# Loading the first chunk of a softmax in four parts instead of two

## The chip, the cores and the metric

The kernel runs on one core of a Trainium2 chip. A core has compute engines with a queue of instructions each (here VectorE, written DVE; ScalarE, ACT; GpSimd, POOL; and SyncE, SP, which here only issues transfers) and 16 DMA engines that move data between device memory (HBM) and the on-chip memory (SBUF, 128 partitions). The metric is the time of one execution on the device in microseconds; lower is better. Times of a kernel are given as the median of several runs.

## The reference

The input is 16 x 1024 rows of 512 float32 numbers. Each row gets a softmax at temperature 0.5:

```python
temp = 0.5
x_scaled = x / temp
x_max = np.max(x_scaled, axis=-1, keepdims=True)
exp_x = np.exp(x_scaled - x_max)
return (exp_x / np.sum(exp_x, axis=-1, keepdims=True)).astype(np.float32)
```

33.55 MB are read and 33.55 MB written.

## The kernel before

The 16384 rows are cut into C = 8 chunks of 2048 rows. In a chunk, each of the 128 partitions holds G = 16 successive rows of 512 numbers, 32 KB, which lie together in HBM as well. A chunk is 4 MB. Six chunks fit in SBUF (`BUFS`, line 42); chunks 6 and 7 reuse the memory of chunks 0 and 1, so their loads wait for those chunks' stores.

Transfers and computing are cut differently. `LOADS` (line 38) says in which groups of rows a chunk is loaded, `BLOCKS` (line 39) in which groups it is computed. Chunk 0 is loaded in two parts (rows 0 to 3, rows 4 to 15) and computed in three blocks (rows 0 to 3, 4 to 7, 8 to 15). The middle chunks are loaded and computed whole. Chunk 7 is loaded without its last row, which the GpSimd queue loads later (`load_last_row`, lines 88 to 100), and computed in two blocks. Every chunk is stored whole, by one DMA from the ACT queue (line 148).

For a block, `shift` (line 71) has DVE take the maximum of every row, negated (line 77), and double it (line 81). `exponentials` (line 102) has ACT compute exp(2x - 2max) for one row per partition at a time and add it up (line 108). `scale_vector` (line 120) has DVE take reciprocals of the sums (line 125) and multiply the rows by them (line 127); in blocks of eight rows or more, one row in eight is scaled by ACT instead (line 138). `store` (line 144) stores a chunk once its last block is scaled.

The order is written out by hand (lines 154 to 172). DVE's order is: maxima of block 0, maxima of block 1, then for each block i its scaling, and the maxima of block i + 2. Loads are issued by SP from within `shift`, the first time that a chunk is touched; as nothing holds the loads of chunks 0 to 5, SP issues them one after the other at the start. A reduction waits for every load that wrote something it reads: before the change, block 0 waits for the first part of chunk 0, blocks 1 and 2 for the second.

At the end an SP instruction (line 174) collects the completion of every transfer in `finished`.

Of the kernel before, what the change touches and what calls it, by code (L numbers as in the profile page):

```python
# [1 line left out]

# [4 lines left out]


@with_exitstack
def kernel(  # L10
    ctx: ExitStack,
    tc: tile.TileContext,
    x: bass.AP,
    out: bass.AP,
):
    nc = tc.nc
    fp32 = mybir.dt.float32
    P = nc.NUM_PARTITIONS
    AX = mybir.AxisListType.X
    EXP = mybir.ActivationFunctionType.Exp  # L20
    COPY = mybir.ActivationFunctionType.Copy
    MAX = mybir.AluOpType.max

    D = x.shape[-1]
    xf = x.flatten_outer_dims()
    of = out.flatten_outer_dims()
    N = xf.shape[0]

    G = 16
    C = N // (P * G)
    assert C * P * G == N
    xr = xf.rearrange("(c p g) d -> c p g d", p=P, g=G)
    outr = of.rearrange("(c p g) d -> c p g d", p=P, g=G)
    WHOLE = [(0, G)]
    LOADS = [[(0, 4), (4, G)]] + [WHOLE] * 6 + [[(0, G - 1)]]
    BLOCKS = [[(0, 4), (4, 8), (8, G)]] + [WHOLE] * 6 + [[(0, 8), (8, G)]]
    STORES = [WHOLE] * 8  # L40
    BMAX = 16
    BUFS = 6

    data = ctx.enter_context(tc.tile_pool(name="data", bufs=BUFS))
    stats = ctx.enter_context(tc.tile_pool(name="stats", bufs=6))

    ctx.enter_context(tc.manual_schedule())


    warm = stats.tile([P, 1], fp32, name="warm", bufs=1)  # L50
    nc.vector.memset(warm, 0.0)  # L51
    nc.scalar.activation(out=warm, in_=warm, func=EXP)  # L52

    chunks = {}
    blocks = [(c, lo, hi) for c in range(C) for lo, hi in BLOCKS[c]]
    n = len(blocks)
    biases, sums, recips = {}, {}, {}

    finished = []

    def load(c):
        if c < BUFS:
            chunks[c] = data.tile([P, G, D], fp32, name="xt")
        else:
            chunks[c] = chunks[c - BUFS]
        xt = chunks[c]
        for lo, hi in LOADS[c]:
            part = nc.sync.dma_start(out=xt[:, lo:hi, :], in_=xr[c][:, lo:hi, :])  # L68
            finished.append(part.ins.name)

    def shift(i):
        c, lo, hi = blocks[i]
        if c not in chunks:
            load(c)
        b = hi - lo
        negmax = stats.tile([P, BMAX], fp32, name="negmax")
        nc.vector.tensor_reduce(  # L77
            negmax[:, 0:b], chunks[c][:, lo:hi, :], axis=AX, op=MAX, negate=True
        )
        biases[i] = stats.tile([P, BMAX], fp32, name="bias")  # L80
        nc.vector.tensor_scalar_mul(biases[i][:, 0:b], negmax[:, 0:b], 2.0)  # L81

    def load_last_row(signal):
        seen = stats.tile([P, 1], fp32, name="seen", bufs=1)
        copied = nc.gpsimd.tensor_copy(out=seen, in_=signal)  # L90
        finished.append(copied.ins.name)
        c = C - 1
        halves = "p (h d) -> p h d"
        to = chunks[c - BUFS][:, G - 1, :].rearrange(halves, h=2)
        of_ = xr[c][:, G - 1, :].rearrange(halves, h=2)
        for p0, p1 in ((P - 2, P), (0, P - 2)):
            part = nc.gpsimd.dma_start(  # L97
                out=to[p0:p1], in_=of_[p0:p1], max_dma_last_dim=2 * D
            )
            finished.append(part.ins.name)  # L100

    def exponentials(i, rows):
        c, lo, hi = blocks[i]
        if i not in sums:
            sums[i] = stats.tile([P, BMAX], fp32, name="sums")
        for g in rows:
            row = chunks[c][:, lo + g, :]
            nc.scalar.activation(  # L108
                out=row,
                in_=row,  # L110
                func=EXP,
                bias=biases[i][:, g : g + 1],
                scale=2.0,
                accum_out=sums[i][:, g : g + 1],
            )
            if c == BUFS - 1 and g == 10:
                load_last_row(sums[i][:, g : g + 1])


    def scale_vector(i):  # L120
        c, lo, hi = blocks[i]
        b = hi - lo
        k = b - b // 8
        recips[i] = stats.tile([P, BMAX], fp32, name="recip")
        nc.vector.reciprocal(recips[i][:, 0:b], sums[i][:, 0:b])  # L125
        rows = chunks[c][:, lo : lo + k, :]
        last = nc.vector.tensor_mul(  # L127
            rows, rows, recips[i][:, 0:k].unsqueeze(2).broadcast_to((P, k, D))
        )
        if i == n - 1:  # L130
            finished.append(last.ins.name)

    def scale_scalar(i):
        c, lo, hi = blocks[i]
        b = hi - lo
        for g in range(b - b // 8, b):
            row = chunks[c][:, lo + g, :]
            last = nc.scalar.activation(  # L138
                out=row, in_=row, func=COPY, scale=recips[i][:, g : g + 1]
            )  # L140
            if i == n - 1:
                finished.append(last.ins.name)

    def store(i):
        c, _, end = blocks[i]
        for lo, hi in STORES[c]:
            if hi == end:
                part = nc.scalar.dma_start(
                    out=outr[c][:, lo:hi, :], in_=chunks[c][:, lo:hi, :]
                )  # L150
                if c < C - 1:
                    finished.append(part.ins.name)

    shift(0)
    shift(1)

    def rows(i):
        c, lo, hi = blocks[i]
        cut = hi - lo - (2 if c == 1 else 0)
        return range(cut), range(cut, hi - lo)  # L160

    exponentials(0, rows(0)[0])
    for i in range(n):
        if i + 1 < n:
            exponentials(i + 1, rows(i + 1)[0])
        scale_vector(i)
        scale_scalar(i)
        if i + 2 < n:
            shift(i + 2)
        store(i)  # L170
        if i + 1 < n:
            exponentials(i + 1, rows(i + 1)[1])

    seen = nc.sync.nop()
    info = mybir.DependencyInfo(
        mybir.DependencyClass.Sync, mybir.DependencyReason.DATA
    )
    for name in finished:
        tc.add_manual_dep(seen.ins, name, info, reason="leaves one wait for the end")


# [1 line left out]
_INS = ['x']  # L183
_OUTS = [((16, 1024, 512), 'float32')]


# [23 lines left out]
```

## Time and profile before

| what | value |
|---|---|
| median of 3 runs | 161.78 us (161.74 to 161.98) |
| the profiled execution | 162.29 us, span 160.5 us |
| DVE busy | 134.6 us |
| ACT busy | 102.2 us |
| bytes moved | 67.13 MB, mean 418 GB/s |
| first load, 1 MB: issue to landing | 4.8 us |
| second load, 3 MB: issue to landing | 11.6 us |

The span runs from the first instruction to the last of one execution; the time of the execution contains a little more. A page of the profile gives the busy time of each engine, the span in 40 slices with the busy share in tenths, the DMA queues (q1 is SP's, q10 ACT's, q0 GpSimd's), and the chain of waits that ended last. A "releaser" after an arrow is what ended an engine's wait. A number like L77 is a line of the kernel. A 128x4 in an instruction is partitions by elements.

### The profile page before, as it was taken

The numbers are of one execution on the slowest core, as the hardware profiler recorded it, in microseconds if no ns is written. First come the engines' busy times: TensorE is split into PE (matmuls) and PEld (weight loads), VectorE is DVE, ScalarE is ACT, GpSimd is POOL, SyncE is SP. The second block draws the span as 40 slices with busy tenths as digits, with TensorE's granted clock in tenths as the row PEclk, the third lists the DMA queues.
The fourth block names the chain that finished last, engine by engine and source line by source line (L and its number), as shares of the span: only waits on it lengthen the run. The fifth ranks groups of instructions, "written<-read, shape, count | busy, mean of one in ns | idle before, by whom it ended". The sixth has DMA issues, their size and how long they took to land.

```text
span 160.5 us, 411 instructions
## 1 busy us (share of the span) xinstructions
DVE 134.6 (84%) x45; ACT 102.2 (64%) x273; POOL 1.9 (1%) x7
## 2 busy tenths in 40 slices
DVE  0607999999999999999999999999999999957000
ACT  3071549069989963998199909991899891790000
POOL 0000000000000000000000000030000000000000
DMA  5999999999989999999999999989999999999994
GB/s 184 470 408 498 400 392 457 457 392 402 506 269 425 490 392 400 506 400 392 490 425 392 474 434 392 490 383 483 422 450 400 400 465 441 392 457 449 400 441 204
DMA packets 2578, 67.13 MB, mean 418 GB/s; under 512 B 328, under 2 KB 328, under 8 KB 400
## 3 DMA queue, kind: packets, MB, share of 16 engines
q1 hardware_dynamic: 1296, 33.29, 49.3%
q10 hardware_dynamic: 1152, 33.55, 48.4%
q0 software_dynamic: 128, 0.26, 0.4%
q14 instruction: 2, 0.02, 0.0%
HBM read 33.55 MB, written 33.55 MB: 418 GB/s over the span
## 4 chain that ended last, share of the span: by engine, by line
DVE 75%; DMA 7%; issue 5%; ACT 3%; SPq 0%
DVE negmax L77 42%; DVE xt L127 31%; DMA xt<-in_x_dram 7%; ACT xt L108 3%; DVE bias L81 1%; DVE recip L125 1%; SPq L68 0%
## 5 line engine op out<-in xcount | busy, mean ns | idle before, releaser
L108 ACT ACTIVATE xt<-xt,bias 128x512 f32<-128x512 f32 x128 | 90.4, 708 | 41.5 <-DVE bias L81 40.6
L77 DVE TENSOR_REDUCE negmax<-xt 128x16 f32<-128x8192 f32 (+2 forms) x11 | 69.9, 6352 | 9.4 <-DMA xt<-in_x_dram 9.4
L127 DVE TENSOR_TENSOR xt<-xt,recip 128x7168 f32<-128x7168 f32 (+2 forms) x11 | 62.0, 5637 | 0.4
L108 ACT ACTIVATION_READ_ACCUMULATOR xt<-xt,bias 128x1 f32 x128 | 23.9, 187 | 0.0
L138 ACT ACTIVATE xt<-xt,recip 128x512 f32<-128x512 f32 x15 | 9.9, 706 | 0.0
L125 DVE RECIPROCAL recip<-sums 128x16 f32<-128x16 f32 (+2 forms) x11 | 2.4, 218 | 1.8 <-ACT xt L108 1.8
L81 DVE TENSOR_SCALAR bias<-negmax 128x16 f32<-128x16 f32 (+2 forms) x11 | 1.9, 173 | 0.4
L52 ACT ACT_TABLE_LOAD x1 | 1.3, 1283 | 0.7 <-PEq L194 0.7
L97 POOL DMA_DIRECT2D xt<-in_x_dram x2 | 1.5, 741 | 0.5 <-issue 0.5
L90 POOL COPY seen<-sums 128x1 f32<-128x1 f32 x1 | 0.2, 184 | 103.6 <-ACT xt L108 103.6
L51 DVE MEMSET warm<- 128x1 f32 x1 | 0.1, 59 | 0.8 <-PEq L194 0.8
L52 ACT ACTIVATE warm<-warm 128x1 f32<-128x1 f32 x1 | 0.2, 202 | 0.0
L194 POOL MEMSET const-float32-0.0<- 128x1 f32 x1 | 0.1, 93 | 0.2 <-issue 0.2
L194 POOL MEMSET const-bfloat16-1.0<- 128x1 bf16 x1 | 0.1, 95 | 0.0
L194 POOL MEMSET const-uint8-127<- 128x1 uint8 x1 | 0.1, 95 | 0.0
L194 POOL MEMSET const-float32-1.0<- 128x1 f32 x1 | 0.1, 93 | 0.0
## 6 DMA issues: line engine op xcount, KB each, us to landing
out_dram<-xt ACTq DMA_DIRECT2D x8, 4096.0 KB, 23.1
xt<-in_x_dram SPq DMA_DIRECT2D x6, 4096.0 KB, 34.8
xt<-in_x_dram SPq DMA_DIRECT2D x1, 3840.0 KB, 27.8
xt<-in_x_dram SPq DMA_DIRECT2D x1, 3072.0 KB, 11.6
xt<-in_x_dram SPq DMA_DIRECT2D x1, 1024.0 KB, 4.8
xt<-in_x_dram POOLq DMA_DIRECT2D x1, 252.0 KB, 15.4
xt<-in_x_dram POOLq DMA_DIRECT2D x1, 4.0 KB, 9.1
```

Source lines behind the costliest of these rows:

```text
L51: nc.vector.memset(warm, 0.0)
L52: nc.scalar.activation(out=warm, in_=warm, func=EXP)
L77: nc.vector.tensor_reduce(negmax[:, 0:b], chunks[c][:, lo:hi, :], axis=AX, op=MAX, negate=True)
L81: nc.vector.tensor_scalar_mul(biases[i][:, 0:b], negmax[:, 0:b], 2.0)
L90: copied = nc.gpsimd.tensor_copy(out=seen, in_=signal)
L97: part = nc.gpsimd.dma_start(out=to[p0:p1], in_=of_[p0:p1], max_dma_last_dim=2 * D)
L108: nc.scalar.activation(out=row, in_=row, func=EXP, bias=biases[i][:, g : g + 1], scale=2.0, accum_out=sums[i][:, g : g + 1],)
L125: nc.vector.reciprocal(recips[i][:, 0:b], sums[i][:, 0:b])
L127: last = nc.vector.tensor_mul(rows, rows, recips[i][:, 0:k].unsqueeze(2).broadcast_to((P, k, D)))
L138: last = nc.scalar.activation(out=row, in_=row, func=COPY, scale=recips[i][:, g : g + 1])
L194: nc = _bacc.Bacc("TRN2", target_bir_lowering=False, num_devices=1)
```

## The change

The first chunk gets a list of loads of its own, in which a load may take some of the partitions only. In order: partitions 0 to 15 with rows 0 to 7 (16 KB each); partitions 16 to 127 with rows 0 to 3 (8 KB each); partitions 16 to 127 with rows 4 to 15 (24 KB each); partitions 0 to 15 with rows 8 to 15 (16 KB each). The blocks that are computed stay as they are, so block 0 (rows 0 to 3) now reads what the first two loads wrote, block 1 (rows 4 to 7) what the first and the third wrote, and block 2 (rows 8 to 15) what the third and the fourth wrote. All other loads are as before.

```diff
-    LOADS = [[(0, 4), (4, G)]] + [WHOLE] * 6 + [[(0, G - 1)]]
+    LOADS = [WHOLE] * 7 + [[(0, G - 1)]]
     BLOCKS = [[(0, 4), (4, 8), (8, G)]] + [WHOLE] * 6 + [[(0, 8), (8, G)]]
     STORES = [WHOLE] * 8
+    FIRST = [(0, 16, 0, 8), (16, P, 0, 4), (16, P, 4, G), (0, 16, 8, G)]
...
         xt = chunks[c]
-        for lo, hi in LOADS[c]:
-            part = nc.sync.dma_start(out=xt[:, lo:hi, :], in_=xr[c][:, lo:hi, :])
+        parts = FIRST if c == 0 else [(0, P, lo, hi) for lo, hi in LOADS[c]]
+        for p, q, lo, hi in parts:
+            part = nc.sync.dma_start(
+                out=xt[p:q, lo:hi, :], in_=xr[c][p:q, lo:hi, :]
+            )
             finished.append(part.ins.name)
```

## The prediction

> **What bounds the kernel now.** I read the page first for what is full, then the chain of waits, then stretches of the span at both ends.
>
> ```profile
> span 160.5 us, 411 instructions
> ...
> DVE 134.6 (84%) x45; ACT 102.2 (64%) x273; POOL 1.9 (1%) x7
> ...
> DMA  5999999999989999999999999989999999999994
> ...
> q1 hardware_dynamic: 1296, 33.29, 49.3%
> q10 hardware_dynamic: 1152, 33.55, 48.4%
> q0 software_dynamic: 128, 0.26, 0.4%
> ...
> DVE 75%; DMA 7%; issue 5%; ACT 3%; SPq 0%
> ```
>
> The chain names DVE for 75% of the span, but the queue lines say more: their packets fill 49.3 + 48.4 + 0.4 = 98.1% of the span of 16 DMA engines. One engine's rate follows from the store queue: 33.55 MB / (0.484 x 16 x 160.5 us) = 27.0 GB/s, so 16 engines make 432 GB/s and the kernel's 67.1 MB cannot take less than 67.1 / 0.432 = 155.3 us. The span is 160.5.
>
> ```profile
> core 0: us, DVE busy (x) ACT busy (x) POOL busy (x), PEclk, DMA share, GB/s
> 1.00:2.00 1.00, 0.00 (x0) 1.00 (x1) 0.00 (x0) 1.00 0.66 106
> 2.00:3.00 1.00, 0.00 (x0) 0.22 (x2) 0.00 (x0) 1.00 0.58 197
> 3.00:12.00 9.00, 2.46 (x2) 2.93 (x8) 0.00 (x0) 1.00 1.01 432
> ...
> 148.00:158.00 10.00, 0.00 (x0) 0.00 (x0) 0.00 (x0) 1.00 1.05 455
> 158.00:160.50 2.50, 0.00 (x0) 0.00 (x0) 0.00 (x0) 1.00 0.00 0
> ```
>
> The second to last column is the DMA share (packets that straddle an edge make it pass 1). The engines start at about 1.7 us, are slow for one microsecond, full from 3 us, and full again up to 158 us, when all computing has ended. What they lose anywhere in between moves the end by as much.
>
> ```profile
> 5.52 2.29 DVE L77 TENSOR_REDUCE negmax<-xt 128x4 f32<-128x2048 f32 x1 [4.65 <-DMA xt<-in_x_dram]
> ...
> 12.80 2.29 DVE L77 TENSOR_REDUCE negmax<-xt 128x4 f32<-128x2048 f32 x1 [4.79 <-DMA xt<-in_x_dram]
> ...
> 17.61 4.41 DVE L77 TENSOR_REDUCE negmax<-xt 128x8 f32<-128x4096 f32 x1
> ...
> 24.55 8.68 DVE L77 TENSOR_REDUCE negmax<-xt 128x16 f32<-128x8192 f32 x1
> ...
> 147.48 0.34 ACTq L148 DMA_DIRECT2D out_dram<-xt  x1
> ```
>
> This is the timeline (start, duration). DVE waits twice, for the two loads of the first chunk, and then runs without a gap over 0.1 us from 12.80 to 137.3 us. The last store is issued at 147.48. The store before it lands between 148.8 and 150.0 us (landings of its 16 engines), so the engines are still busy with it, and DVE's path has little slack, between nothing and about 1 us. So two paths end nearly together: the DMA's total work, and DVE from 12.80 us on. The first is the later one.
>
> [...]
>
> **The change part by part.**
>
> Removed: two loads of 128 partitions, 1.05 and 3.15 MB. Added: four loads, 0.26 MB (16 partitions x 16 KB), 0.92 MB (112 x 8 KB), 2.75 MB (112 x 24 KB), 0.26 MB (16 x 16 KB). Bytes are the same. Only chunk 0's loads change; everything else keeps its place in its queue.
>
> Issue. SP issues two more DMAs at about 0.4 us each (the row of line 68: 327 / 425 / 667 ns minimum, median, maximum), ahead of the loads of chunks 1 to 5. Chunk 1's load goes out about 0.85 us later, near 2.5 us, and its data is not due before 12 us. Hidden. The second part goes out near 1.15 us, before the first part's data flows at 1.74. Hidden. Two more completion marks per engine: taken as nothing, below 0.1 us.
>
> Part 1. At full rate 0.26 MB takes 0.61 us. [...] Lower bound: [...]0, and even a gain[...]; that gain cannot pass the slow start, which is 0.65 us (at 27.0 GB/s an engine's first 64 KB would take 2.4 us, its data ran from 1.74 to about 4.85, so 3.1 less 2.4). I take +1.8.
>
> Parts 2 and 3. Seven partitions an engine; which ones no run shows. The nearest assumption is seven in a row: engine e has 16 + 7e to 22 + 7e. [...] At full rate the parts take 3.67 MB / 0.432 = 8.5 us: +1.8 us on average[...], +3.6 us for the worst. Lower bound 0. Upper bound: neighbouring partitions handed to different engines in turn[...], +25 us. [...]
>
> Part 4. As part 1 if the engines come to it together, +1.8; less if parts 2 and 3 have set them apart: about +1.0. I take +1.4 on average, +1.0 beside the worst engine's delay.
>
> Sum for the DMA engines: 1.8 + 1.8 + 1.4 = +5.0 us on average, 1.8 + 3.6 + 1.0 = +6.4 us for the worst engine. Every later load and store of 128 partitions gives each engine equal work, so a late engine stays late to the end and the end waits for the last. [...] I take +5.4.
>
> DVE's path. The first reduce now needs parts 1 and 2: 1.8 us of part 1, 0.3 us for 0.13 MB more, and a share of part 2, so it starts near 8 us instead of 5.52. It and its exponentials (until 10.98 before) had 1.8 us to spare before 12.80, and the second reduce moves too. The second needs parts 1 to 3 and no longer part 4: 12.80 + 1.8 + 1.8 - 0.6 (0.26 MB not waited for) = 15.8, up to 17.5 behind the worst engine. That is +3.0 to +4.7, and the last store is issued by that much later; the engines are free for it 5.0 to 6.4 us later. So the DMA engines stay the later path. The third reduce needs part 4, before at 17.61, now 20.6 or later, with part 4 in by about 18.1 on average (12.8 + 5.0, and a little): covered. Chunk 1 would land near 22.5 + 5.4 = 27.9 for a reduce due at 24.55 + 3.9 = 28.5: just covered, and if not, DVE only moves closer to the DMA path.
>
> Against the profiled execution: 160.5 + 5.4 = 165.9 us span; its time is 162.29 us, 1.8 beyond the span, so 167.7. The median of the runs, 161.78, is 0.5 below: **167.2 us**.
>
> **Rivals.**
>
> A, forecast, 0.47: [...]166.0 to 168.6.
>
> B, 0.27: [...] 161.8 + 1.8 + (1.0 to 1.8) = 164.6 to 165.4; smaller still, 163, if half of that is absorbed. [...]
>
> C, not slower, 0.19: [...] Then the bytes are the same and full engines leave room for the start alone[...]. That also moves DVE's start from 12.80 to 12.2, so its path would not stand in the way. 161.2 to 161.8, with 161.4 in the middle. It decides as soon as part 1's data is through in under about 1.2 us from its first packet. For it: the 1 us at 106 and 197 GB/s is a real loss. [...]
>
> D, 0.04: partitions in turn over the engines, 190 us.
>
> E, 0.03: the split does not do what it says because the second reduce still waits for all four loads: it adds 0.6 us to DVE's path only, and A's time stands, at 167.
>
> **How the numbers follow.** Likeliest: 167.2. The range leaves out C and D, 0.23, but takes a little of the soft side of B: 162.9 to 169.6. What the measurement can tell from no change is 0.2%, 0.3 us. Slower: A, B, D, E, and 0.01 of C: 0.82. The rest of C splits into 0.13 faster and 0.05 within.
>
> **What would show it.** Right: the first reduce starts at 7.5 us or later, the second at 15 to 17.5 us; DMA in the stretch 3 to 12 us well under 432 GB/s while its share stays near 1; the last store issued near 151. Parts 2 and 3 alone: the second load's landing beyond 2.1 us after the first's. Wrong: the second reduce at 12.2 to 12.8 us with 432 GB/s from 3 us on; then C holds, and what decides is how soon the engines fill before 3 us.

## The result, and the profile after

The changed kernel takes 169.75 us (median of 5 runs, 169.41 to 170.2), the kernel before 161.78 us. The ratio is 1.0496, 95% interval 1.0475 to 1.0517: 8.0 us slower. The prediction had the direction right, and that these loads of a part of the partitions are slow, but the size too small: it said 167.2 us, and the measured time lies just above its range. Its charges for the four loads (+1.8 us for part 1, +1.8 to +3.6 for parts 2 and 3, +1.4 for part 4) were its author's estimate; no trace of the kernel before shows such loads.

The page after, with the lines that answer those of before:

```profile
span 167.5 us, 415 instructions
...
DVE 134.6 (80%) x45; ACT 102.2 (61%) x273; POOL 1.9 (1%) x7
...
DMA  6999999898999999999999999989899999999994
GB/s 102 291 270 280 184 438 438 383 493 376 471 407 462 415 438 438 430 438 399 477 391 477 391 469 399 477 383 470 384 440 476 391 462 415 454 422 430 446 422 196
...
q1 hardware_dynamic: 1328, 33.29, 51.3%
q10 hardware_dynamic: 1152, 33.55, 46.4%
...
DVE 72%; DMA 11%; issue 5%; ACT 3%; SPq 0%
```

No compute engine works longer than before: DVE still 134.6 us, ACT 102.2. The digits of the DMA row are as full as before. The row below them tells the difference: slices 2 to 5 (4.2 to 21 us) move 184 to 291 GB/s with the engines marked busy. So DMA engines that are marked busy need not move data at their full rate. The same in stretches; the last two columns are DMA share and GB/s:

```profile
core 0: us, DVE busy (x) ACT busy (x) POOL busy (x), PEclk, DMA share, GB/s
1.00:2.00 1.00, 0.00 (x0) 1.00 (x1) 0.00 (x0) 1.00 0.59 115
2.00:3.00 1.00, 0.00 (x0) 0.22 (x2) 0.00 (x0) 1.00 0.96 180
3.00:12.00 9.00, 2.46 (x2) 1.18 (x3) 0.00 (x0) 1.00 1.04 273
12.00:22.00 10.00, 2.53 (x3) 1.80 (x7) 0.00 (x0) 1.00 1.00 249
22.00:46.00 24.00, 23.83 (x10) 14.53 (x41) 0.00 (x0) 1.00 1.00 432
```

From 3 to 12 us, 273 GB/s stand where there were 432; from 22 us on, when loads of 128 partitions are all that is left, the rate is 432 again. The timeline of the reductions and of the last store:

```profile
8.30 2.29 DVE L83 TENSOR_REDUCE negmax<-xt 128x4 f32<-128x2048 f32 x1 [7.43 <-DMA xt<-in_x_dram]
...
19.43 2.29 DVE L83 TENSOR_REDUCE negmax<-xt 128x4 f32<-128x2048 f32 x1 [8.64 <-DMA xt<-in_x_dram]
...
24.24 4.41 DVE L83 TENSOR_REDUCE negmax<-xt 128x8 f32<-128x4096 f32 x1
...
31.18 8.68 DVE L83 TENSOR_REDUCE negmax<-xt 128x16 f32<-128x8192 f32 x1
...
154.11 0.34 ACTq L154 DMA_DIRECT2D out_dram<-xt  x1
```

The second reduction starts at 19.43 us instead of 12.80, and everything DVE does afterwards keeps that distance: the last store is issued at 154.11, 6.63 us later. The store before it lands between 155.8 and 157.0 us on its 16 engines, so the engines are still behind DVE, as predicted.

Landings of the last engine say how much each part cost. Part 1 landed at 5.12 us. At full rate it would have landed at 5.50 - 1.82 = 3.68, since before 1.05 MB landed at 5.50 and 0.79 MB less takes 1.82 us less: +1.4. Part 2 came 3.08 us after it, for 2.12 at full rate; part 3 11.21 us later, for 6.37; together +5.8. Part 4 came 2.06 us after that, for 0.61: +1.45. Chunk 1 followed in 9.36 us, for 9.71: -0.35. The sum is +8.3, and chunk 1 lands at 30.83 us, before at 22.51.

### The profile page after: what moved, and what is told of

Same layout as the page of the kernel before. It is cut to its first block, busy times and chain, and to the rows that moved or that the text cites. A ratio compares the mean times of both kernels' runs of the same rounds, so it can differ in the third digit from the quotient of the medians.

```text
span 167.5 us, 415 instructions
## 1 busy us (share of the span) xinstructions
DVE 134.6 (80%) x45; ACT 102.2 (61%) x273; POOL 1.9 (1%) x7
## 4 chain that ended last, share of the span: by engine, by line
DVE 72%; DMA 11%; issue 5%; ACT 3%; SPq 0%
DVE negmax L83 40%; DVE xt L133 30%; DMA xt<-in_x_dram 11%; ACT xt L114 3%; DVE bias L87 1%; DVE recip L131 1%; SPq L72 0%
```

## The experiments

**Only the number and sizes of the loads (four_wide).** Kernel before, chunk 0 in four loads over all partitions:

```diff
-    LOADS = [[(0, 4), (4, G)]] + [WHOLE] * 6 + [[(0, G - 1)]]
+    LOADS = [[(0, 1), (1, 4), (4, 15), (15, G)]] + [WHOLE] * 6 + [[(0, G - 1)]]
```

> Chunk 0 in four loads of about the same sizes as the change (1, 3, 11 and 1 rows), but each over all 128 partitions. If the narrow partition ranges are what costs: within 0.5 us of before (161.8). If the number of loads, their issue or a small first load costs: at least 2 us slower.

Measured: 162.64 us against 161.83, ratio 1.0052 (1.0033 to 1.007). The count, the issue and a small first load together cost 0.8 us here, a little more than the 0.5 expected (the interval starts at 0.53), and far less than the change's 8.0. If costs add, which was not tested, the narrow ranges of partitions bring the rest. Little of the 0.8 is lost at the start: chunk 1 lands at 22.77 us, before at 22.51. The last store lands over 1.9 us on its 16 engines, before over 1.2, so the engines end less evenly.

**DVE earlier (three_wide).** Three loads over all partitions, so that the second reduction needs only the second megabyte:

```diff
-    LOADS = [[(0, 4), (4, G)]] + [WHOLE] * 6 + [[(0, G - 1)]]
+    LOADS = [[(0, 4), (4, 8), (8, G)]] + [WHOLE] * 6 + [[(0, G - 1)]]
```

> Chunk 0 in three loads over all 128 partitions, rows 0-3, 4-7, 8-15, so that the second reduction waits for 1 MB and not for 3. DVE's second reduction starts near 7.8 us instead of 12.8. If the DMA engines' total work sets the end: within 0.7 us of before. If DVE's start does: about 4 to 5 us faster, up to where the DMA engines stop it.

Measured: 162.24 us against 161.83, ratio 1.0022 (1.0014 to 1.003). The second reduction started at 8.16 us, 4.64 us sooner, and the kernel was no faster (by the interval 0.2 to 0.5 us slower). The DMA engines' work sets the end of the kernel before; what the change could have won for DVE (0.26 MB less to wait for, 0.6 us) was never to be had.

**What a narrow load costs, in a stream (rates).** Extra loads ahead of the kernel before, a 2-row load of 128 partitions after each; the first two of them:

```diff
+    to, src = fill(5, slice(0, 128), 0, 2)
+    nc.sync.dma_start(out=to, in_=src)
+    to, src = fill(0, slice(0, 128), 0, 8)
+    nc.sync.dma_start(out=to, in_=src)
+    to, src = fill(5, slice(0, 128), 2, 4)
+    nc.sync.dma_start(out=to, in_=src)
+    to, src = fill(0, slice(16, 128), 8, 16)
+    nc.sync.dma_start(out=to, in_=src)
...
```

> The kernel before, with nine extra loads ahead of it (rows of 16 KB into chunks that are loaded properly later), each followed by a 128-partition load of 2 rows that clears the engines (1.21 us). Cost of a load = landing of its follower less the landing of the follower before, less 1.21 us. At full rate: 128 partitions 4.85 us, 112 partitions 4.25, 96 partitions (32 to 127) 3.64, 64 partitions 2.43, 32 partitions 1.21, 16 partitions 0.61. Theory 1, [...]shares are partitions in a row: 0-63 and 0-31 twice their full-rate time (4.85, 2.43), 0-15 four times (2.4), but 32-95 at full rate (2.43) though it has no more partitions than 0-63, 16 partitions in steps of 7 under 1.5, 112 partitions 5.4 to 6.7. Theory 2, [...]partitions handed out in turn: 32-95 as slow as 0-63 and both well over 4.85, 112 partitions far over 6.7. Rival, [...]any load of fewer than 128 partitions or of few descriptors an engine is slow: 0-63 equal to 32-95, and 0-15 equal to the steps of 7.

Measured, by the follower's landing (last engine): 16-127 took 7.4 us and 0-111 7.0, for 4.25 at full rate; 32-127 7.2 for 3.64; 0-63 5.05 for 2.43; 0-31 2.4 for 1.21; 0-15 2.7 and 16 partitions in steps of seven 1.8, for 0.61. Partitions 32-95, as many as 0-63, landed 2.5 us after what was ahead of them: full rate. By their follower, the measure of the others, they took 3.9 us; the follower itself came in slowly, ahead of the load of 0-15. Either way 32-95 is not equal to 0-63, nor 0-15 to the steps of seven, as the rival wants; the loads taken alone, below, show it without followers. The run also showed the weak place: 112 partitions cost 1.65 to 1.74 times their time, more than theory 1 expected (5.4 to 6.7 us).

**The same in other ranges (rates2).** As rates, with the ranges named in its expectation.

> As rates, other ranges; full-rate times in brackets. 36-99 and 48-111 with 32 KB a partition (4.85 each), 8-119 (4.25), 16-111 (3.64), 32-79 (1.82), 64-111 (1.82), 16-95 (3.03), 16 KB each. [...] Theory 1a, [...]36-99 moves near 400 GB/s for its first 4.85 us and only two engines are late; costs of the others[...]: 8-119 5.1, 16-111 4.8, 16-95 3.8. Theory 1b, [...]36-99 moves near 216 to 280 GB/s throughout and costs 7.5 to 9.7, and the others go toward twice the full-rate time: 8-119 7 to 8.5, 16-111 7.3, 16-95 6, 32-79 3.6.

Inconclusive as a measurement: 36-99 landed 14.4 us after its forerunner, where 9.7 was the most expected and the load taken alone, below, cost 9.8. So in this stream the costs ran into each other. Its first load was clean: after the start-up, packets of 32 KB on all but two engines took 1.2 to 1.4 us, those of the two 2.5 and more. So in this load only two engines were held back, as theory 1a expected.

**Each load alone (alone, alone2).** To part them, 16 extra loads of 32 KB a partition go into the same memory, so that each is issued when the one before has landed:

```diff
+    part = slice(0, 128)
+    nc.sync.dma_start(out=made[0][part], in_=xr[0][part])
+    part = slice(16, 128)
+    nc.sync.dma_start(out=made[0][part], in_=xr[0][part])
...
```

> The kernel before, with 16 extra loads ahead of it, 32 KB a partition, each into the same memory so that each is issued only when the one before has landed. Time of a load = next issue less its own issue; about 2 us of it are start and landing, the rest is data. Data at full rate: 128 partitions 9.7 us, 112 8.5, 96 7.3, 80 6.1, 64 4.85, 48 3.6, 16 1.2. If every share is partitions in a row[...], the last engine's data is done after: 112 partitions 11.7, 96 12.4, 80 11.0, 32-79 5.3, 0-47 10.1, 48 in steps of two 6.1, 32-95 5, 0-63 10, 64 in steps of two 10, 0-15 5, steps of seven 2.6. If shares that are no power of two (7, 6, 5, 3) are handed out in turn instead: 112, 96 and 80 over 20 us, 0-47 and 32-79 both 14, 48 in steps of two 7.4. [...]as the rates run suggests for 112 and 96: 112 about 14 to 15, 96 about 14.4, 80 about 11 to 12.

> As alone, other ranges, in this order: 128; 64 in steps of two from 1; 32-95; 36-99; 48-111; 16-111; 8-119; 24-103; 48-95; 48 in steps of two from 32; 32 in steps of two from 0; 0-31; 32 in steps of four; 16 in steps of eight; 16 in steps of four; 128. Data at full rate: 9.7, 4.85, 4.85, 4.85, 4.85, 7.3, 8.5, 6.1, 3.6, 3.6, 2.4, 2.4, 2.4, 1.2, 1.2, 9.7. Three theories of what holds a load back beyond its own bytes. In a row[...]: 36-99 9.7 with only two engines late, 48-111 9.7 with half of the packets at 1.2 us, 64 from 1 9.9, 32 in steps of four 5.0, 48-95 5.1, 16-111 12.0, 8-119 11.2. [...] Uneven shares (no power of two) hold back all engines: 48-95 7, 48 in steps of two 7, 24-103 11.5, 16-111 14, 8-119 14, every packet alike, while 48-111 still has fast and slow packets.

SP's queue in the timeline of alone, where the distance of two issues is the time of the earlier load:

```profile
0.75 0.37 SPq L64 DMA_DIRECT2D xt<-in_x_dram  x1
13.03 0.34 SPq L66 DMA_DIRECT2D xt<-in_x_dram  x1
30.33 0.32 SPq L68 DMA_DIRECT2D xt<-in_x_dram  x1
...
140.94 0.52 SPq L84 DMA_DIRECT2D xt<-in_x_dram  x1
148.37 0.50 SPq L86 DMA_DIRECT2D xt<-in_x_dram  x1
161.04 0.51 SPq L88 DMA_DIRECT2D xt<-in_x_dram  x1
168.65 0.32 SPq L90 DMA_DIRECT2D xt<-in_x_dram  x1
175.10 0.53 SPq L92 DMA_DIRECT2D xt<-in_x_dram  x1
```

All 128 partitions (issued at 0.75) took 12.28 us, of which 9.71 are data at 432 GB/s; the other 2.5 are taken off every load below, which makes those times estimates. Then 16-127, with fewer bytes, took 17.30 us. Partitions 32-95 (issued at 140.94) took 7.43 us, 0-63 after it 12.67, every second partition of 128 7.61, and 0-15 (issued at 168.65) 6.45.

| partitions | share of an engine | less 2.5 us | at full rate | ratio |
|---|---|---|---|---|
| 32-95 | 4 | 4.9, 5.0 | 4.85 | 1.0 |
| even, odd ones of 128 | 4 | 5.1, 5.0 | 4.85 | 1.0 |
| 0-63 | 4 | 10.2 | 4.85 | 2.1 |
| 36-99 | 4 | 9.8 | 4.85 | 2.0 |
| 48-111 | 4 | 9.9 | 4.85 | 2.0 |
| 32 in steps of four | 2 | 2.6 | 2.4 | 1.05 |
| 0-31 | 2 | 4.6 | 2.4 | 1.9 |
| 0-15 | 1 | 3.95 | 1.2 | 3.3 |
| 16-127 | 7 | 14.8 | 8.5 | 1.74 |
| 0-111 | 7 | 13.7 | 8.5 | 1.61 |
| 8-119 | 7 | 15.7 | 8.5 | 1.85 |
| 32-127, 0-95 | 6 | 14.0, 14.3 | 7.3 | 1.9, 2.0 |
| 16-95 | 5 | 11.2 | 6.1 | 1.84 |
| 32-79 | 3 | 7.0 | 3.6 | 1.9 |

The share is the partitions divided by 16, and the time at full rate is the share at 1.21 us for each 32 KB, the median packet of that size in the kernel before. In the changed kernel a load has one packet for each partition (16 of 16 KB, 112 of 24 KB) and lands 16 times; that the loads here are divided as evenly is an estimate.

A load need not have all 128 partitions to move at full rate: 32-95 and the even partitions move at about 420 GB/s (2.10 MB in 4.9 to 5.1 us). 0-63, with as many partitions and bytes, moves at half of that: 193 GB/s from 150 to 159 us, where 32-95 has 393 from 143 to 147. Nor is it enough to spread the partitions: 32 of them in steps of two from 0 (alone2) took 7.54 us, less 2.5 about 5.0, for 2.4 at full rate. What tells the fast ranges from the slow ones was not shown.

With shares of 3, 5, 6 or 7 every load in the table took 1.6 to 2.0 times its full-rate time. Neither order that the expectations took gives that: for partitions in a row 5.1 us were expected of 48-95 (measured 6.8) and 11.2 of 8-119 (15.7); for partitions handed out in turn, over 20 of 16-127 (14.8).

In a row fails for some even shares too: its expectation was 10 us for every second partition (measured 5.1 and 5.0) and 5.0 for 32 in steps of four (2.6). What came nearly true are the times that the expectation of alone took over from rates, which describe and do not explain: 112 partitions 14 to 15, 96 14.4, 80 11 to 12. In the loads with these shares no packet ran at its full-rate 1.21 us: the fastest took 1.42, and the median was 2.0 to 2.5 (4.0 for 0-47). But alone2 cuts both ways. Two stretches in it, the middle of 36-99 and of 48-111:

```profile
30.00:34.00 4.00, 0.00 (x0) 0.00 (x0) 0.00 (x0) 1.00 0.96 385
42.00:52.00 10.00, 0.00 (x0) 0.00 (x0) 0.00 (x0) 1.00 0.80 167
```

36-99 moves 385 GB/s in this stretch; in rates2 only two engines were slow in it. In 48-111, with the same share, the rate is 167 GB/s, the fastest packet took 1.52 us and all after each engine's first took 2.5, twice the full-rate time; the expectations by shares in a row and by uneven shares had fast packets there. So slow packets on all engines are not a matter of uneven shares only. Why they come with some ranges and not with others, and which engine gets which partition, stays open: no run here shows an engine's partitions.

**Does lost DMA time move the end one for one? (halves, middle, combs, split32)** The change's list with other partitions:

```diff
-    FIRST = [(0, 16, 0, 8), (16, P, 0, 4), (16, P, 4, G), (0, 16, 8, G)]
# halves
+    FIRST = [(0, 64, 0, 4), (64, P, 0, 4), (0, 64, 4, G), (64, P, 4, G)]
# middle
+    FIRST = [(32, 96, 0, 4), (0, 32, 0, 4), (96, P, 0, 4)]
+    FIRST += [(32, 96, 4, G), (0, 32, 4, G), (96, P, 4, G)]
# combs, with a step of 2 in both partition slices
+    FIRST = [(0, P, 0, 4), (1, P, 0, 4), (0, P, 4, G), (1, P, 4, G)]
# split32
+    FIRST = [(0, 32, 0, 8), (32, P, 0, 4), (32, P, 4, G), (0, 32, 8, G)]
```

> Chunk 0 in four loads of 64 partitions (0-63 and 64-127, rows 0-3, then rows 4-15)[...]. If time lost by the DMA engines at the start moves the end one for one: 4.19 MB at half rate, 9.7 us lost, 171.5 us. If a part of it is hidden later or DVE's path sets the end: clearly under 170 or over 173.

> Chunk 0 in six loads, 32-95, 0-31, 96-127 for rows 0-3 and again for rows 4-15. [...]4.85 us lost, 166.6 us, faster than halves by 4.9 with more loads and narrower ones. If what costs is the number of partitions or of loads[...]: as slow as halves or slower.

> As halves (four loads of 64 partitions for chunk 0, rows 0-3, then 4-15), but the even partitions and the odd ones in place of 0-63 and 64-127[...]. [...]nothing lost, 161.8 to 162.8 us (four_wide, with as many loads, 162.6). If loads of fewer than 128 partitions cost by their number or width: near halves, 172.

> The change with 32 and 96 partitions in place of 16 and 112: shares of two and six. By the costs measured in rates (32 partitions twice, 96 partitions twice their full-rate time) the first chunk loses 2.4 + 7.3 = 9.7 us: 171.5 us. By the sharing that the prediction used[...] 2.4 + 2.4 to 4.9: 166.6 to 169.1.

| kernel | us | before beside it | ratio, 95% interval |
|---|---|---|---|
| halves | 172.01 | 161.86 | 1.0627 (1.0611 to 1.0643) |
| middle | 167.94 | 161.86 | 1.0384 (1.0364 to 1.0404) |
| combs | 163.36 | 161.97 | 1.0084 (1.0066 to 1.0103) |
| split32 | 170.47 | 161.79 | 1.053 (1.0512 to 1.0547) |

Halves and combs have the same number of loads, of partitions and of bytes; only which partitions go together differs, and 8.65 us lie between them. So what the change pays for is its choice of partitions, not the number or width of its loads.

On which side of the transfer the time goes was not shown: every load here takes partition p from the same place of its chunk in device memory, 32 KB times p from the start, so all runs change the partitions and the addresses read together. No run loads a partition from another place.

Chunk 0 in even and odd partitions costs 1.4 us (combs), in 0 to 63 and 64 to 127 it costs 10.1 (halves).

Halves came 0.5 us over its expectation, middle 1.3, combs 0.6; split32 lies between its two theories. In halves, middle and combs the other path took over, so they do not answer the question. Stretches of middle near the end, and its last store:

```profile
152.00:153.00 1.00, 1.00 (x1) 0.00 (x0) 0.00 (x0) 1.00 0.61 262
153.00:154.00 1.00, 0.52 (x1) 0.00 (x0) 0.00 (x0) 1.00 0.01 0
154.00:155.00 1.00, 0.00 (x0) 0.00 (x0) 0.00 (x0) 1.00 1.22 524
```

```profile
153.60 0.34 ACTq L155 DMA_DIRECT2D out_dram<-xt  x1
```

The DMA engines run dry, and no packet of data starts between 153 and 154 us, because DVE is not ready before 153.60. Middle's second reduction started at 18.93 us, 6.1 later than before, and its median is 6.1 us longer: it had to wait for all of chunk 0, while the DMA engines had lost less. In combs the second reduction started at 14.61 us, 1.8 later, and the last store left 1.8 us later, at 149.30.

Halves, which came out near its expectation, did so by DVE's path too, which is luck. Its second reduction started at 23.28 us, 10.5 later than before, as did its last store, and just ahead of that store's data no packet starts for 1 us:

```profile
157.70:158.70 1.00, 0.16 (x1) 0.00 (x0) 0.00 (x0) 1.00 0.01 0
```

```profile
157.95 0.34 ACTq L154 DMA_DIRECT2D out_dram<-xt  x1
```

The change and split32 answer better, as there the DMA engines stay behind DVE to the end: when chunk 1 lands they have lost 8.3 and 9.5 us, and the spans are 7.0 and 8.0 us longer. So the loss moves the end one for one but for 1.3 to 1.5 us, which the last section takes up.

## Why the prediction was right and wrong

What bounds the kernel: right. The DMA engines' total work ends last, before (three_wide) and after (last store issued at 154.11, engines busy with the one before until 155.8 to 157.0).

Issue and number of loads, "below 0.1 us": too low if the change pays what four_wide does, 0.8 us for two more loads and their sizes; its own landings, above, add up without it.

Part 1, +1.8: measured +1.4. Part 4, +1.4 on average or +1.0: measured +1.45. That a load of partitions 0 to 15 is slow, and slower than one of as many others, is shown by alone: 3.95 us for 0-15, 2.2 for 16 partitions in steps of seven, where both are 1.2 at full rate. The prediction's +1.8 on 0.61 us is four times the full-rate time; 0-15 alone took 3.3 times, and 2.3 x 0.61 us is the 1.4 measured for part 1. So the +1.4 for part 4 was met by luck: the prediction took it for +1.8, made less by engines set apart.

**The step that failed is the term for parts 2 and 3**: "+1.8 us on average", "+3.6 us for the worst". It measured +5.8 us, 14.3 where 8.5 is full rate, a factor of 1.68; the same 112 partitions alone have 1.74. The step was the author's estimate: an assumed order, seven partitions in a row, and a slowing that follows from it, neither of which any run shows. In the runs no engine kept its full rate with a share of seven: in the changed kernel no packet of part 3 took less than 1.17 us, where 24 KB at full rate take 0.91, and the median was 1.46. Why, was not shown. With 5.8 in the place of 1.8 to 3.6, and the measured parts 1 and 4 and chunk 1, the sum is 8.3.

"I take +5.4", below the worst engine's +6.4: the wrong way. In rates2, where loads follow each other, the costs did not soften either: 36-99 landed 14.4 us after its forerunner, and alone cost 9.8. The upper bound of +25 us held and was far off.

DVE's path: the first reduction "near 8 us" came at 8.30. The second, "15.8, up to 17.5", came at 19.43, by the same missing term. That parts 4 and chunk 1 would be covered was right: neither reduction waits.

Of the signs that were named, three came: the first reduction after 7.5 us, a rate well under 432 GB/s at a share near 1 from 3 to 12 us (273 at 1.04), and the second load landing more than 2.1 us after the first (3.08). The second reduction (19.43 for at most 17.5) and the last store (154.11 for near 151) came later than named.

Of the rivals, B (only the two 16-partition loads cost anything) is excluded by rates and alone (112 partitions took 1.6 to 1.85 times their full-rate time), C by the rate from 3 to 12 us, D by its size. E's premise is not what happened either: the second reduction starts at 19.43, and part 4 lands at 21.47.

From the profiled execution to the median: the spans differ by 7.0 us, the medians by 8.0. Before, the profiled execution was 0.5 us above its median; after, it took 169.6 us, 0.15 below its own, and lay 2.1 us beyond its span for 1.8. And 1.3 us of the 8.3 lost by chunk 1's landing do not show in the spans; the last section says where they are.

## What to carry to other kernels

When the DMA engines are full to the end, ask of every split of a load which partitions go together: in even and odd ones chunk 0 cost 1.4 us more (combs), in 0 to 63 and 64 to 127 10.1 (halves), and 0 to 15 alone took 3.3 times its full-rate time. The profile can show the engines as busy all the while (share 1.04 at 273 GB/s in the changed kernel, 3 to 12 us). Read GB/s beside the DMA share, not the share. A mean from an assumed order is a poor price for an irregular pattern (+1.8 us forecast for parts 2 and 3, +5.8 measured); measure such a load alone before you build on it.

## What was not expected of the hardware

A load with a share of 3, 5, 6 or 7 partitions an engine took 1.6 to 2.0 times its full-rate time (0-47 took 3.2 times, 11.6 us for 3.6), where the prediction's +1.8 to +3.6 on 8.5 us makes 1.2 to 1.4 for a share of seven.

The kernel before loses about 1.2 us when its first store begins. Its stretches from 44 us on, and below them those of the changed kernel around its own first store (issued at 50.7 us):

```profile
44.00:46.00 2.00, 2.00 (x1) 1.55 (x5) 0.00 (x0) 1.00 0.78 311
46.00:48.00 2.00, 1.93 (x4) 1.73 (x6) 0.00 (x0) 1.00 1.09 262
48.00:50.00 2.00, 2.00 (x1) 2.00 (x7) 0.00 (x0) 1.00 1.07 459
```

```profile
50.00:54.00 4.00, 3.93 (x4) 3.27 (x9) 0.00 (x0) 1.00 0.91 393
54.00:58.00 4.00, 4.00 (x1) 4.00 (x13) 0.00 (x0) 1.00 1.06 459
58.00:62.00 4.00, 4.00 (x2) 4.00 (x11) 0.00 (x0) 1.00 1.04 451
```

Before, the mean from 44 to 50 us is 344 GB/s, a fifth under 432; after, it is 434 from 50 to 62. This is the 1.2 us by which the spans differ less than the landings of chunk 1. Three_wide (344) and four_wide (382) dip in the same stretch; halves (434) and middle (437) do not from 50 to 62 us, nor does split32 (451 from 52 to 60). In before's dip packets of the loads take up to 2.5 us for 1.21; in the changed kernel from 50 to 54 us none takes over 1.22. What stalls there was not tried.
